# A float32 decoder trunk on one core: first products no longer parted, small steps of feed-forward entries and ends re-ordered, mask building split around the opening

## The chip, the cores and the metric

The kernel runs on one core of one Trainium2 chip. The metric is the device time of one execution in microseconds; "time before" is the median of three runs. Beside the runs there is one profiled execution with its trace, from which all durations come. Engines: PE is TensorE's matmul, PEld its weight load, DVE is VectorE, ACT is ScalarE, POOL is GpSimd, SP is SyncE, which issues most transfers. "L316" is line 316 of the kernel before.

## The reference, cut to what matters

Two layers over 512 tokens of width 1024, in float32. Each layer has two feed-forwards around a token mixer, so there are four feed-forwards:

```
def swiglu(h, w_in, w_out):                      # w_in 1024 x 5632, w_out 2816 x 1024
    gate, up = jnp.split(h @ w_in, 2, axis=-1)
    return (jax.nn.silu(gate) * up) @ w_out

for l in range(DEPTH):                           # DEPTH = 2
    x = x + 0.5 * swiglu(rms_norm(x, ffn1_norm[l]), ffn1_w_in[l], ffn1_w_out[l])
    h = rms_norm(x, mix_norm[l]) @ w_mix_in[l]
    ...                                          # short convolution, HGRN2, forgetting attention
    x = x + y @ w_mix_out[l]
    x = x + 0.5 * swiglu(rms_norm(x, ffn2_norm[l]), ffn2_w_in[l], ffn2_w_out[l])
```

## The kernel before, in words

**Precision.** Every float32 operand is kept as two parts, a rounded high part (`hi`, `xh`) and the remainder (`lo`, `xl`), both of the type float32r. A product of two operands is three matmuls (`mm3`): hi x high at L316, hi x low at L322, lo x high at L323. The high part is a ScalarE copy, the low part a VectorE subtraction.

**A feed-forward** (`ffn`) treats the 2816 hidden columns in 22 blocks of 128. The first four (six in the first feed-forward) are "covered": computed directly with 512-column matmuls (`stream_steps`, weights through `granule` and `parted`), while the norm is finished. The rest goes through `halved`, a Strassen-like scheme in which each 2 x 2 block product takes seven products instead of eight. A unit `("I", w)` is two input blocks of the gate and the up matrix, with products in the order `ORDER_IN = P1, P2, P6, P5, P7, P3, P4`; a unit `("O", ...)` is an output product for a finished chunk of hidden blocks. Each product is 24 matmuls of 256 columns. `CHUNKS` are blocks 0 to 7, 8 to 15 and 16 to 21; `plan` writes down the order of all products and when each load, DMA addition, `total` (a VectorE sum) and `moving` part is done.

**Order in `halved`.** For product number n the loop issues its matmuls (`product`), then `prepare` for product n + 3 (ScalarE high part, L784; the VectorE low part, L786, is kept for later as `rest`), then what is done with the finished bank, then `rest()`, for the last chunk the rounding of the hidden values (L934 on ScalarE, L935 on VectorE), then `run(n)` (the plan's steps; sums at L772) and what `self.entry` holds for n. `A`, `V`, `G` and `S` chain these instructions (`follow`), so ScalarE, VectorE and the queues take them in the order written; the matmuls are chained too (`keep`). Of the bank work: P1 is copied off at L886, P2 subtracted at L889, P6 copied off at L895 (in feed-forwards with an entry this copy, L870, already stands ahead of `prepare`), P5 copied at L898, P7 added at L901, P3 at L904; P4's product gives the hidden values. P1, P6, P7 and P4 of a unit use one bank.

**Parted products.** The first matmul of P1 is split into two of 128 columns for the covered chunk's first unit and the first unit of each later chunk.

**Entry** (`enter`, three of four feed-forwards): it interleaves the direct matmuls with the norm and with the halves of x for P1 to P7 (`high` at L606, `low` at L609 or L611). What does not fit is left in `self.entry` under the product number after which it is issued.

**Opening** (`cover` with `open_stream`, first feed-forward): x is loaded, turned by TensorE (L1686), scaled (`scaled`, L389 and L390) and multiplied with the first weights (L1749), whose parts are made at L1705 and L1706. `idle` issues small matmuls on zeros (L1723). `build_consts` makes the masks for the mixer on VectorE; it stands after `open_stream` in the program, unchained, and the scheduler that orders the unchained instructions puts its steps wherever it expects room. The norm's sum is at L419 and L428.

**Way out** (`way_out`, last feed-forward): the last chunk's hidden blocks times `w_out`, 512 columns at a time into banks that already hold x; the very last tile is halved into two of 256 columns.

Of the kernel before, what the change touches and what calls it, by code (L numbers as in the profile page):

```python
# [23 lines left out]
P = 128  # L24
# [17 lines left out]

SKEW_HELD, SKEW_MOVING = 16, 48
EPS = 1e-6
CH = 64
# [111 lines left out]
class Trunk:  # L157
# [8 lines left out]
    def __init__(self, ctx, tc):  # L166
# [20 lines left out]
        self.tab, self.tab_users, self.loaded = None, [], None  # L187
        self.chain = {}

    def build_consts(self, scratch):  # L190
# [35 lines left out]
        nc.vector.tensor_tensor(later, ftf, ptf, op=ALU.is_gt)  # L226
        a = scratch(F32)[:, :P]
        b = scratch(F32)[:, :P]
        for l in range(1, 7):
            nc.vector.tensor_scalar(a, xf, scalar1=float(2 ** (l - 1)), scalar2=None, op0=ALU.is_ge)  # L230
            nc.vector.tensor_scalar(b, xf, scalar1=float(2**l), scalar2=None, op0=ALU.is_lt)
            nc.vector.tensor_mul(a, a, b)
            for par in range(2):
                r = slice(CH * par, CH * par + CH)
                nc.vector.tensor_mul(self.lmask[r, l - 1, :], a[r, r], later[r, r])

        nc.vector.tensor_scalar(self.maskb, later, scalar1=-1e30, scalar2=None, op0=ALU.mult)

        nc.vector.tensor_tensor(self.utri[:, :P], ftf, ptf, op=ALU.is_ge)
        of = scratch(F32)[:, P:]  # L240
        nc.vector.memset(of, 1.0)
        nc.vector.tensor_copy(self.utri[:, P:], of)

# [35 lines left out]

    def granule(self, parts, kk, ahead=True, skew=0, keep=False, queued=False):  # L280
# [30 lines left out]

    def mm3(self, acc, ah, al, bh, bl, first, last, parted=False, keep=False):
        nc = self.nc
        n = bh.shape[-1]
        for c in (slice(0, n // 2), slice(n // 2, n)) if parted else (slice(0, n),):
# [4 lines left out]
            if keep:  # L320
                self.follow("p", i)
        nc.tensor.matmul(acc, ah, bl, start=False, stop=False, skip_group_check=True)  # L322
        i = nc.tensor.matmul(acc, al, bh, start=False, stop=last, skip_group_check=True)  # L323
        if keep:
# [5 lines left out]

    def stream_steps(self, jobs, parts_of, act, nk, mid=None, pre=None, given=None, queued=False):
        k = 0
        while k < nk:
# [3 lines left out]
            if pre is not None:  # L337
                pre(k)
            skew = SKEW_MOVING if jobs[0][2] is not None and jobs[0][0].shape[-1] < T else 0
            keep = given is not None and given(k)  # L340
            rows = self.granule(parts_of(k, kk), kk, pre is None, skew, keep, queued)
            if keep:
                yield
            end = k + kk == nk
            order = (
# [143 lines left out]
    def cover(self, fp, w_in, covered, begin, then):  # L489
        nc = self.nc  # L490
        x, gain, logits = begin
        for f in range(0, covered, 2):
# [20 lines left out]
            if opening:  # L513
                self.open_stream(x, gain, fp, parts, jobs)
            else:
                self.stream([(*j, None) for j in jobs], parts, self.xact, KD, queued=f == 2)
            if opening:
                nt = iter(["xh4", "xl4", "xh5", "xl5", "xh6", "xl6", "r2", "r3", "r4", "r5"])
                self.build_consts(lambda dt: fp.tile([P, T], dt, tag=next(nt), name=self.n("c")))
                norm()  # L520
# [36 lines left out]
    def enter(self, fp, w_in, then):  # L557
# [74 lines left out]
        def values(f, i):  # L632
# [107 lines left out]
    def halved(self, fp, w_in, w_out, covered):  # L740
# [67 lines left out]
        def product(u, p, bank, start, stop, parted):  # L808
            hi, lo = parts.pop((u, p))
            xh, xl = self.xc[p] if u[0] == "I" else mov[u[1][0], p]  # L810
            for i in range(2):
                acc, c = bank[:, i * H : (i + 1) * H], slice(i * P, (i + 1) * P)
                for k in range(4):
                    self.mm3(
                        acc, hi[:, k, c], lo[:, k, c], xh[:, k, :], xl[:, k, :],
                        start and i == 0 and k == 0, stop and i == 1 and k == 3,
                        parted and i == 0 and k == 0, True,
                    )

# [30 lines left out]
        used = {"I": 0, "O": 0}  # L850
        work = {}

# [4 lines left out]
        for n, (kind, w, p) in enumerate(seq):  # L857
# [3 lines left out]
            if p in new:  # L861
# [3 lines left out]
                u, p, acc, p in new, p in ("P2", "P3", "P4"),  # L865
                kind == "I" and p == "P1" and w in (covered, *(f0 for f0, _ in CHUNKS)),
            )
            if kind == "I" and p == "P6" and self.entry and w == covered:
                work[u, "g2"] = g2 = tmp("g2")
                A(nc.scalar.activation(g2, acc, AF.Copy, scale=-1.0))  # L870
# [35 lines left out]
            else:  # L906
# [8 lines left out]
                else:  # L915
# [13 lines left out]
                    self.hh.append(hh)  # L929
                    self.hl.append(hl)  # L930
            if rest is not None:
                rest()
            if kind == "I" and p == "P4" and w >= CHUNKS[2][0]:
                A(nc.scalar.copy(hh, y))  # L934
                V(nc.vector.tensor_sub(hl, y, hh))  # L935
# [701 lines left out]
    def way_out(self, w_out, out, f0, nf):  # L1637
        nc = self.nc
        for dg in range(2):
            banks = self.next4()  # L1640
            jobs = []
            for i, bk in enumerate(banks):
                t = slice(i * P, (i + 1) * P)
                for q in range(4):
# [12 lines left out]

            self.stream(jobs, parts, self.last_hidden, nf)
            for n, (bk, c, t, _) in enumerate(jobs):
                o = self.res.tile([P, T], F32, tag=f"x{(4 * dg + n) % 8}", name=self.n("xo"))  # L1660
# [8 lines left out]

    def open_stream(self, x, gain, fp, parts, jobs):  # L1670
        nc = self.nc
# [30 lines left out]

        def part(s3, hl, j):
            hi, lo = (hl[:, a + 512 * j : a + 512 * j + 512] for a in (0, 1024))
            A(nc.scalar.copy(hi, s3[:, j, :]))  # L1705
            V(nc.vector.tensor_sub(lo, s3[:, j, :], hi))  # L1706
            return hi, lo
# [3 lines left out]
        V(nc.vector.memset(zeros, 0.0))  # L1711
        A(nc.scalar.dma_start(rows, gain.rearrange("(k p) -> k p", p=P)))
        self.gain = self.const.tile([P, KD], F32, tag="gain", name=self.n("gain"), bufs=2)
# [13 lines left out]
        A(nc.scalar.copy(self.gain, gb[:, :KD]))  # L1727
        idle(2)
        turn(0)
        idle(2)  # L1730
        for k in range(0, KD, 2):
# [5 lines left out]
            wh = []  # L1737
            def make(j):
                self.norm_part(k + j, fp, xb[k + j], 0)
                wh.append(part(*w, j))  # L1740

# [83 lines left out]
```

## Time and profile before

| | us |
|---|---|
| median of 3 runs | 1816.66 (1815.56 to 1819.09) |
| profiled execution | 1815.31 |
| its span in the trace | 1813.2 |
| TensorE matmul busy | 1801.3 (99%) |
| VectorE busy | 1461.3 (81%) |
| ScalarE busy | 1001.0 (55%) |
| HBM read, over the span | 223.98 MB, 125 GB/s |

Timeline rows are: start in the span, duration, engine, line, operation, out<-in, shapes, count. A bracket at the end gives the engine's idle time before it and what ended it. The ends of matmuls are modelled: one of 256 columns is shown with 0.28 us although the next can start 0.11 us after it. Starts are what to read.

The first feed-forward takes the span up to about 340 us (its halved stage from 76.8 to 306.8), then the mixer to about 578, the second feed-forward to about 910 (halved stage from 627.7 to 876.8); the second layer follows in the same way, with halved stages from 953.5 and 1523.3, and the last feed-forward ends the span.

### The profile page before, as it was taken

How to read it: one execution, taken by the hardware profiler on the slowest of the kernel's cores; microseconds unless marked ns; L12 is line 12 of the kernel's file. 1: busy time of each engine (PE TensorE's matmuls, PEld its weight loads, DVE VectorE, ACT ScalarE, POOL GpSimd, SP SyncE). 2: the span in 40 equal slices, each digit the busy share in tenths (PEclk: the TensorE clock that was granted, in tenths of full speed). 3: DMA queues.
4: the chain of work that ended last, by engine and by line, in shares of the span. 5: the costliest groups of instructions: out<-in, count | busy, mean ns of one | idle time of the engine just before them, and what ended most of it. 6: DMA issues, size and time to landing. Idle time of an engine off the chain costs nothing.

```text
span 1813.2 us, 34777 instructions
## 1 busy us (share of the span) xinstructions
PE 1801.3 (99%) x14281; PEld 1682.8 (93%) x14281; DVE 1461.3 (81%) x2048; ACT 1001.0 (55%) x1434; POOL 170.3 (9%) x172
## 2 busy tenths in 40 slices
PE   9999999999999999999999999999999999999999
PEld 7899999899878899999889999998998788999997
DVE  9889787676887898889678887976868878888883
ACT  5455555464775565555445555555547755555551
POOL 0011120100000001112001111201000000020210
PEclk9999999999999999999999999999999999999999
DMA  6768783233323757868275787823233237687762
GB/s 197 186 135 191 179 175 96 74 79 85 87 82 105 216 136 161 197 159 168 82 207 130 163 193 192 163 68 79 77 90 86 82 102 212 163 158 192 158 134 93
DMA packets 243934, 250.94 MB, mean 138 GB/s; under 512 B 18456, under 2 KB 229152, under 8 KB 243776
## 3 DMA queue, kind: packets, MB, share of 16 engines
q1 hardware_dynamic: 189872, 182.38, 33.3%
q0 software_dynamic: 53600, 66.09, 22.8%
q8 instruction: 112, 1.84, 0.4%
q14 instruction: 46, 0.38, 0.1%
q10 hardware_dynamic: 304, 0.27, 0.0%
HBM read 223.98 MB, written 2.10 MB: 125 GB/s over the span
## 4 chain that ended last, share of the span: by engine, by line
PE 91%; DVE 5%; ACT 3%; issue 1%; DMA 0%; SPq 0%; ACTq 0%; DVEq 0%
PE mm L316 13%; PE mm L323 13%; PE mm L322 13%; PE sc L323 6%; PE sc L316 6%; PE sc L322 6%; PE pt L316 6%; PE pt L322 6%; PE pt L323 6%; PE po L316 4%; PE po L322 4%; PE po L323 4%; PE po L1581 1%; PE pt L1623 1%; ACT hl L305 1%
## 5 line engine op out<-in xcount | busy, mean ns | idle before, releaser
L784 ACT CAST hl<-w 128x1024 fp32r<-128x1024 f32 x322 | 337.1, 1049 | 318.2 <-PE mm L323 78.1
L786 DVE TENSOR_TENSOR hl<-w,hl 128x1024 fp32r<-128x1024 f32 x322 | 392.6, 1222 | 85.4 <-ACT hl L784 85.3
L306 DVE TENSOR_TENSOR hl<-st,hl 128x512 fp32r<-128x512 f32 (+2 forms) x188 | 161.6, 860 | 100.7 <-ACT hl L305 99.8
L305 ACT CAST hl<-st 128x512 fp32r<-128x512 f32 (+2 forms) x188 | 141.8, 754 | 176.8 <-PE po L323 62.3
L316 PE MATMUL mm<-xc,hl 128*128 128x256 f32 (+1 forms) x732 | 201.6, 276 | 0.5 <-ACT g L895 0.5
L323 PE MATMUL mm<-xc,hl 128*128 128x256 f32 x728 | 201.4, 277 | 0.0
L322 PE MATMUL mm<-xc,hl 128*128 128x256 f32 x728 | 201.4, 277 | 0.0
L323 PE MATMUL sc<-xc,hl 128*128 128x256 f32 x528 | 146.3, 277 | 0.0
L316 PE MATMUL sc<-xc,hl 128*128 128x256 f32 (+1 forms) x530 | 146.3, 277 | 0.0
L322 PE MATMUL sc<-xc,hl 128*128 128x256 f32 x528 | 146.2, 277 | 0.0
L316 PEld LDWEIGHTS mm<-xc,hl 128*128 128x128 f32 x732 | 137.4, 188 | 0.9 <-ACT g L895 0.7
L323 PEld LDWEIGHTS mm<-xc,hl 128*128 128x128 f32 x728 | 136.7, 188 | 0.1
L322 PEld LDWEIGHTS mm<-xc,hl 128*128 128x128 f32 x728 | 136.7, 188 | 0.0
L322 PE MATMUL pt<-xc,hl 128*128 128x256 f32 x480 | 133.0, 277 | 0.0
L316 PE MATMUL pt<-xc,hl 128*128 128x256 f32 (+1 forms) x484 | 133.0, 276 | 0.0
L323 PE MATMUL pt<-xc,hl 128*128 128x256 f32 x480 | 132.8, 277 | 0.0
L316 PE MATMUL mm<-x,hl 128*128 128x512 f32 x272 | 107.4, 395 | 0.0
L323 PE MATMUL mm<-x,hl 128*128 128x512 f32 x272 | 106.5, 392 | 0.4 <-DVE hl L306 0.4
L322 PE MATMUL mm<-x,hl 128*128 128x512 f32 x272 | 106.4, 391 | 0.0
L316 PEld LDWEIGHTS sc<-xc,hl 128*128 128x128 f32 x530 | 99.6, 188 | 0.2
L323 PEld LDWEIGHTS sc<-xc,hl 128*128 128x128 f32 x528 | 99.3, 188 | 0.1
L322 PEld LDWEIGHTS sc<-xc,hl 128*128 128x128 f32 x528 | 99.1, 188 | 0.0
(514 smaller groups left out, 5604.9 us busy)
## 6 DMA issues: line engine op xcount, KB each, us to landing
w<-in_ffn_w_in_dram SPq DMA_DIRECT2D x140, 512.0 KB
w<-in_ffn_w_out_dram SPq DMA_DIRECT2D x64, 512.0 KB
w<-in_ffn_w_out_dram POOLq DMA_DIRECT2D x56, 512.0 KB, 9.0
st<-in_w_mix_in_dram SPq DMA_DIRECT2D x88, 256.0 KB
st<-in_ffn_w_in_dram SPq DMA_DIRECT2D x70, 256.0 KB
w<-in_ffn_w_in_dram POOLq DMA_DIRECT2D x35, 512.0 KB, 8.2
w<-S POOLq DMA_DIRECT2D x35, 512.0 KB, 4.7
st<-in_ffn_w_out_dram SPq DMA_DIRECT2D x24, 512.0 KB
```

The source lines that it names most:

```text
L305: a = nc.scalar.copy(hi, src[:, c : c + w])
L306: b = nc.vector.tensor_sub(lo, src[:, c : c + w], hi)
L316: i = nc.tensor.matmul(acc[:, c], ah, bh[:, c], start=first and c.start == 0, stop=False, skip_group_check=True,)
L322: nc.tensor.matmul(acc, ah, bl, start=False, stop=False, skip_group_check=True)
L323: i = nc.tensor.matmul(acc, al, bh, start=False, stop=last, skip_group_check=True)
L784: A(nc.scalar.copy(hi, src))
L786: return lambda: V(nc.vector.tensor_sub(lo, src, hi))
L1581: nc.tensor.matmul(self.ob[:, t0 + u * P : t0 + 2 * P], V[:, j, h % 4].rearrange("p a d -> p (a d)"), part[:, j, u:, :].rearrange("p i t - ...
L1623: nc.tensor.transpose(tb[:, j * P : (j + 1) * P], p[:, j * P : (j + 1) * P], self.ident)
```

## The change

- No product is parted any more (`PARTED = ()`).
- Entry: P4's high part is still made after product 3, but its low part after product 4's bank work and ahead of that product's `rest()` (`self.between`). In that P4 the matmul with the low part of x (hi x low) comes last of each three (`lows`). The clearing of the last direct bank and the values from it come one product later (13 and 14 instead of 12 and 13).
- The copy of P6 ahead of `prepare` for the covered unit also in the first feed-forward.
- Last chunk: the hidden values are rounded four products later, behind an output product; the last ones at once as before.
- Way out: the last tile is halved in its last granule only (`ending`), and that granule's weights lie at another offset (`skew`).
- Opening: `build_consts` is a generator. Its first part (tables, `maskb`, `utri`) is issued ahead of the opening's loads, its second part, the six masks, after `open_stream` and behind the low part of the first weights. A mask takes two instructions on 64 columns instead of five on 128 and 64. The first weights' high part is made on VectorE, behind the tables. One `idle` fewer. The first granule of the next stream (`queued`, k = 0) is chained behind the opening on ScalarE and VectorE.

```diff
+PARTED = ()
...
     def build_consts(self, scratch):
...
+        y = scratch(F32)[:, :CH]
+        for par in range(2):
+            r = slice(CH * par, CH * par + CH)
+            nc.vector.tensor_mul(y[r, :], xf[r, r], later[r, r])
+        nc.vector.tensor_scalar(self.maskb, later, scalar1=-1e30, scalar2=None, op0=ALU.mult)
+        nc.vector.memset(self.utri[:, P:].bitcast(F32), 1.0)
+        i = nc.vector.tensor_tensor(self.utri[:, :P], ftf, ptf, op=ALU.is_ge)
+        self.tables = i.ins.name
+        yield
+        both = [scratch(F32)[:, :CH] for _ in range(2)]
         for l in range(1, 7):
-            nc.vector.tensor_scalar(a, xf, scalar1=float(2 ** (l - 1)), scalar2=None, op0=ALU.is_ge)
-            nc.vector.tensor_scalar(b, xf, scalar1=float(2**l), scalar2=None, op0=ALU.is_lt)
-            nc.vector.tensor_mul(a, a, b)
-            for par in range(2):
-                r = slice(CH * par, CH * par + CH)
-                nc.vector.tensor_mul(self.lmask[r, l - 1, :], a[r, r], later[r, r])
+            b = both[l % 2]
+            i = nc.vector.tensor_scalar(b, y, scalar1=float(2**l), scalar2=None, op0=ALU.is_lt)
+            self.tc.add_manual_dep(i.ins, self.first_low, NOSYNC, reason="given order")
+            nc.vector.scalar_tensor_tensor(
+                out=self.lmask[:, l - 1, :], in0=y, scalar=float(2 ** (l - 1)), in1=b,
+                op0=ALU.is_ge, op1=ALU.mult,
+            )
...
     def granule(...):
-            hi, lo = self.parted(st[:, : kk * c], 1 if ahead else kk, skew, keep)
+            hi, lo = self.parted(st[:, : kk * c], 1 if ahead else kk, skew, keep or first)
...
     def mm3(...):
-        nc.tensor.matmul(acc, ah, bl, start=False, stop=False, skip_group_check=True)
-        i = nc.tensor.matmul(acc, al, bh, start=False, stop=last, skip_group_check=True)
+        rest = [(ah, bl), (al, bh)]
+        (a, b), (c, d) = rest[::-1] if lows else rest
+        nc.tensor.matmul(acc, a, b, start=False, stop=False, skip_group_check=True)
+        i = nc.tensor.matmul(acc, c, d, start=False, stop=last, skip_group_check=True)
...
     def enter(...):
-            3: lambda: both("P4"),
+            3: lambda: high("P4"),
...
-            12: lambda: clear(2, 1),
-            13: lambda: values(2, 1),
+            13: lambda: clear(2, 1),
+            14: lambda: values(2, 1),
         }
+        self.between = {4: lambda: lows["P4"]()}
...
     def halved(...):
-                kind == "I" and p == "P1" and w in (covered, *(f0 for f0, _ in CHUNKS)),
+                kind == "I" and p == "P1" and w in PARTED,
             )
-            if kind == "I" and p == "P6" and self.entry and w == covered:
+            if u == ("I", covered) and p == "P6":
...
+            if n in self.between:
+                self.between.pop(n)()
             if rest is not None:
                 rest()
             if kind == "I" and p == "P4" and w >= CHUNKS[2][0]:
+                final = w + 2 == CHUNKS[2][0] + CHUNKS[2][1]
+                rounded.append((n if final else n + 4, y, hh, hl))
+            if rounded and n >= rounded[0][0] and (kind == "O" or rounded[0][0] == n):
+                _, y, hh, hl = rounded.pop(0)
                 A(nc.scalar.copy(hh, y))
                 V(nc.vector.tensor_sub(hl, y, hh))
...
     def way_out(...):
-                cuts = (0, T) if i < 3 or dg == 0 else (0, T // 2, T)
-                jobs += [
-                    (bk[:, a:b], slice(a, b), t, True) for a, b in zip(cuts, cuts[1:])
-                ]
+                jobs.append((bk, slice(0, T), t, True))
...
+            last = jobs[:3] + halved if dg else jobs
+            self.stream(jobs, parts, self.last_hidden, nf, ending=last)
...
     def open_stream(...):
+            if first:
+                i = nc.vector.tensor_copy(hi, s3[:, j, :])
+                self.tc.add_manual_dep(i.ins, self.tables, NOSYNC, reason="given order")
+                V(i)
+            else:
+                A(nc.scalar.copy(hi, s3[:, j, :]))
...
         V(nc.vector.memset(zeros, 0.0))
+        next(consts)
...
-        idle(2)
+        idle(1)
         turn(0)
         idle(2)
```

`stream_steps` puts the jobs of `ending` in place of its own for the last granule. `product` passes `lows` for P4 of the covered unit where `self.entry` still holds something.

More of the change, by code (lines that the diff above doesn't have):

```diff
@@ L277, in follow, with granule @@
         self.chain[engine] = i.ins.name
-    def granule(self, parts, kk, ahead=True, skew=0, keep=False, queued=False):
+    def granule(self, parts, kk, ahead=True, skew=0, keep=False, queued=False, first=False):
         nc = self.nc
@@ L310, in parted, with mm3 @@
         return hh, ll
-    def mm3(self, acc, ah, al, bh, bl, first, last, parted=False, keep=False):
+    def mm3(self, acc, ah, al, bh, bl, first, last, parted=False, keep=False, lows=False):
         nc = self.nc
@@ L517, in cover @@
             if opening:
[L518 to L519 removed]
+                for _ in consts:
+                    pass
                 norm()
@@ L817, in product @@
                         parted and i == 0 and k == 0, True,
+                        u == ("I", covered) and p == "P4" and bool(self.entry),
                     )
@@ L1738, in make @@
             def make(j):
+                first = k + j == 0
+                if first:
+                    pair, low = part(*w, j, True)
                 self.norm_part(k + j, fp, xb[k + j], 0)
-                wh.append(part(*w, j))
+                if not first:
+                    pair, low = part(*w, j)
+                low()
+                wh.append(pair)
             make(0)
```

48 lines of the change are left out of this document (28 added, 20 removed).

## The prediction

> **What bounds the kernel now.** I read the page first, then the waits, then the timeline of TensorE around every place that the diff touches.
>
> ```profile
> PE 1801.3 (99%) x14281; PEld 1682.8 (93%) x14281; DVE 1461.3 (81%) x2048; ACT 1001.0 (55%) x1434; POOL 170.3 (9%) x172
> ```
>
> TensorE is busy 99% of the 1813.2 us span, so nothing on another engine is worth anything unless it lets a matmul start earlier. But a busy share cannot show a matmul that starts a little late, since one lasts longer than its distance to the next. So I go by starts. This is the halved stage of one feed-forward:
>
> ```profile
> 627.73 0.33 PE L316 MATMUL sc<-xc,hl 128*128 128x128 f32 x2
> 628.07 0.28 PE L323 MATMUL sc<-xc,hl 128*128 128x256 f32 x1
> 630.59 0.28 PE L316 MATMUL sc<-xc,hl 128*128 128x256 f32 x1
> ...
> 644.13 0.19 PEld L316 LDWEIGHTS sc<-xc,hl 128*128 128x128 f32 x1
> 644.19 0.33 PE L316 MATMUL sc<-xc,hl 128*128 128x256 f32 x1
> 644.35 0.28 PE L322 MATMUL sc<-xc,hl 128*128 128x256 f32 x1
> ...
> 666.85 0.33 PE L316 MATMUL pt<-xc,hl 128*128 128x128 f32 x2
> ```
>
> A product is 24 matmuls of 256 columns. From 630.59 to 644.19 five of them, 120 matmuls, take 13.60 us: 113.3 ns each, the full pace. From 644.19 to 666.85 eight, 192 matmuls, take 22.66 us: 118.0 ns each. The second stretch begins with a small slip: 644.35 comes 0.16 after 644.19 instead of 0.11, and from then on TensorE runs 4% slower, with no wait shown. It ends at 666.85, where a parted product stands. At 118 instead of 113.3 ns, 192 matmuls lose 0.90 us. The starts show the same in each of the three feed-forwards that begin with an entry. So the kernel has few long waits, and its losses are slips of 0.05 to 0.7 us and this slower pace.
>
> **The change, part by part.** The sum is made against the profiled execution, 1815.3 us (span 1813.2 and 2.1 around it); the median shown is 1816.7, 1.4 above, and I carry that over at the end.
>
> *Parted products.* The first product of the covered chunk and of the two others is parted in each of four feed-forwards: 12. The one at 627.73 takes 2.86 us to 630.59 against 24 x 0.1133 = 2.72: 0.14 lost, no work hidden by it (its two halves are one matmul's columns). Removed: 12 x 0.135 = 1.6 us. The Trainium skill, TensorE: Matmul & The Clock Gate, section Back-to-back issue gap, gives about 81 ns for a sustained 128-column matmul with its weight load: two would cost 49 ns more than our 113, so 0.6 us in all and a sum of 7.0 instead of 8.0; the trace shows 0.14 each and decides. Bounds: 0 (a wait that the second half now covers appears) to 1.6. But a parted product is also what ended the slower pace at 666.85; this returns as a rival.
>
> *Entry: P4's low part.* VectorE, in front of the slip:
>
> ```profile
> 642.20 1.22 DVE L609 SCALAR_TENSOR_TENSOR xc<-xn,xc 128x1024 fp32r<-128x1024 f32 x1
> 643.33 0.68 DVE L901 TENSOR_TENSOR u<-u,sc 128x512 f32<-128x512 f32 x1
> ```
>
> P4 (from 644.19) adds onto the bank that L901 reads for P7, and L901 ends at 644.01, because P4's own low part (L609) stands before it. Its weight load starts at 644.13, only 0.06 ahead of the matmul where the load is otherwise a full 0.11 ahead: that is the slip. The change turns the two round: L901 then runs 642.2 to 642.9, 1.3 us before it is needed, and L609 about 642.8 to 644.0. What is late next is L609: its result is read by P4's hi x low matmul, which `lows` moves from second to third, at 644.19 + 0.23 = 644.42, its load due at 644.31. Margin 0.3 us, 0.1 to 0.2 after the 0.135 that TensorE comes earlier, if VectorE doesn't follow. Behind L609 only the low part of the product after next waits. Gain: 3 x 0.90 = 2.7 us; bounds 0 to 2.7, below zero only in the rival. The moves of `clear(2, 1)` and `values(2, 1)` by one product put four instructions of VectorE behind P4's own results; the banks they empty are next written five products (13 us) later: nothing.
>
> *First feed-forward: P6's copy ahead of the weights' high part.*
>
> ```profile
> 86.98 1.04 ACT L784 CAST hl<-w 128x1024 fp32r<-128x1024 f32 x1
> 87.74 0.28 PE L323 MATMUL mm<-xc,hl 128*128 128x256 f32 x1
> 87.92 0.58 ACT L895 ACTIVATE g<-mm 128x512 f32<-128x512 f32 x1
> 88.56 0.38 PE L316 MATMUL mm<-xc,hl 128*128 128x256 f32 x1 [0.54 <-ACT g L895]
> ```
>
> L895 frees the bank for P7, due at 87.74 + 0.11 = 87.85; it came at 88.56, 0.71 late, and the matmul after it lost another 0.11. Put first, L895 runs 86.98 to 87.56. Gain 0.8. The high part goes 0.5 later; it is for the product after next. Bounds 0.5 to 0.82.
>
> *Ends: rounding of the hidden values four products later.*
>
> ```profile
> 843.03 1.23 DVE L935 TENSOR_TENSOR hh<-y,hh 128x1024 fp32r<-128x1024 f32 x1
> 845.90 1.22 DVE L772 TENSOR_TENSOR S<-w,w 128x1024 f32<-128x1024 f32 x1
> 848.32 1.23 DVE L786 TENSOR_TENSOR hl<-S,hl 128x1024 fp32r<-128x1024 f32 x1 [1.19 <-ACT hl L784]
> ...
> 849.35 0.28 PE L316 MATMUL sc<-xc,hl 128*128 128x256 f32 x1
> 849.60 0.39 PE L323 MATMUL sc<-xc,hl 128*128 128x256 f32 x1
> 855.08 0.28 PE L316 MATMUL pt<-xc,hl 128*128 128x256 f32 x1
> ```
>
> L786 ends at 849.55 and L323 at 849.60 waits for it; the chain behind it is L935, the sum L772, ScalarE's copy, L786. Two products from 849.35 to 855.08 take 5.73 us against 5.44: 0.29 lost, and alike at the three other ends. Without L935 in front (1.14 from start to start) the sum and L786 come 1.1 earlier, ahead of need. The rounding, with its ScalarE copy, now stands behind an output product's additions, where the next low part has over a product in hand. Gain 4 x 0.25 = 1.0; bounds 0 to 1.15. The last rounding stays where it was.
>
> *Opening, start.* In the fence first TensorE and ScalarE, then VectorE.
>
> ```profile
> 1.22 1.65 PE L1723 MATMUL mm<-z 128*128 128x128 f32 x6 [1.22 <-DVE z L1711]
> 4.02 0.90 PE L1686 MATMUL mm<-ident,xs 128*128 128x128 f32 x4
> 4.76 0.61 PE L1723 MATMUL mm<-z 128*128 128x128 f32 x4
> 4.96 0.69 ACT L389 ACTIVATE x<-mm,gain 128x512 fp32r<-128x512 f32 x1 [1.44 <-PE mm L1686]
> 5.54 0.61 ACT L1705 CAST hl<-st 128x512 fp32r<-128x512 f32 x1
> 6.20 0.73 PE L1749 MATMUL sc<-x,hl 128*128 128x512 f32 x2 [0.84 <-ACT hl L1705]
> ...
> 2.64 0.36 DVE L242 CAST utri<-c 128x384 fp32r<-128x384 f32 x1
> 4.28 0.22 DVE L230 TENSOR_SCALAR c<-c 128x128 f32<-128x128 f32 x1
> 4.55 0.28 DVE L239 TENSOR_TENSOR utri<-c,c 128x128 fp32r<-128x128 f32 x1
> 5.07 0.45 DVE L235 TENSOR_TENSOR lmask<-c,c 64x64 uint8<-64x64 f32 x2
> ```
>
> The first product waits for ScalarE: x, then the weights' high part, done 6.15. With the high part on VectorE only x is left. One `idle` fewer is two small matmuls (`idle(3)` is the six from 1.22), which start 0.21 apart here: 0.43 us, so x is done at 4.96 + 0.69 - 0.43 = 5.22 (at 5.65 if the transposes wait for x's load instead). VectorE must first finish the tables: L239 ends at 4.83, less 0.27 for the cast that goes (L242), less 0.27 for two mask steps (4.28 to 4.55), plus 0.45 for the two multiplies that join the masks (as L235), so 4.74; then the copy, 0.48 scaled from L242 or 0.68 at most: 5.2 to 5.4. Start at 5.3 instead of 6.20: gain 0.9, bounds 0.4 to 0.95. Behind the copy queue x's low part and the weights' low part, wanted four and eight matmuls later (0.9, 1.8 us, and four transposes): covered.
>
> *Opening, end.*
>
> ```profile
> 26.69 1.22 DVE L306 TENSOR_TENSOR hl<-st,hl 128x1024 fp32r<-128x1024 f32 x1
> 27.83 0.74 DVE L390 SCALAR_TENSOR_TENSOR x<-po,gain,x 128x512 fp32r<-128x512 f32 x1
> 27.96 0.50 PE L323 MATMUL mm<-x,hl 128*128 128x512 f32 x1 [0.39 <-DVE hl L306]
> 28.62 0.50 PE L1749 MATMUL sc<-x,hl 128*128 128x512 f32 x1
> 33.79 0.69 DVE L419 TENSOR_TENSOR sh<-sqa,sh 128x512 fp32r<-128x512 f32 x1
> 34.53 0.50 PE L428 MATMUL po<-sh,ones_mean 128*128 128x512 f32 x1
> ```
>
> The next stream's first weights (L306) stand on VectorE ahead of the opening's last x (L390); TensorE waits for the one (0.55), then the other, and for the norm's sum (0.32), with 0.1 to restart after each: 1.3 us. The change puts that granule behind the opening's own chain on ScalarE and VectorE, and the masks fall from 30 instructions to 12, at about 0.2 us each (L230, L235) some 3 us less of VectorE. Then the opening's products run through. Next late is the norm's sum: L419 follows the same chain, and TensorE reaches it 1.8 us earlier. I take 0.9 of 1.3; bounds -0.5 (the granule's low part is wanted before it is done) to 1.3.
>
> *Last tile.* Halved columns only in the last granule: the same columns, 24 matmuls of 256 become 12 of 512, twice as long each. No difference but some slips: 0.1. The other offset of that granule's weights moves addresses only: 0.
>
> Sum: 1.6 + 2.7 + 0.8 + 1.0 + 0.9 + 0.9 + 0.1 = 8.0 us; profiled execution 1807.3, median 1816.7 - 8.0 = 1808.7.
>
> **The rivals.** *A just-late wait sets the slower pace, and nothing ends it.* With no parted products, a slip of 0.05 us in an entry (P4's low part later than 644.3) or at P7 in the first feed-forward (L895 misses 87.74) puts TensorE at 118 ns until the next disturbance; with the ends repaired that may be the end of the chunk, some 200 us on. Price: 200 x 4.7/113.3 = 8.3 us for each feed-forward. It decides from one such stretch: it eats the whole gain. In three entries: 3 x 8.3 = 25, so 1833 or so; in one, 1817. For it: 192 matmuls at 118 ns that ended at a parted product. Against: the margins of 0.1 to 0.3 us, and that after the longer stall at 88.56 the pace was back (seen in the starts). Chance 0.22, half of it one stretch.
>
> *The slips are only exchanged.* P4's slip stays in one form or another but the pace recovers at the next product; the opening gives half: about 4 us, 1812.5. Chance 0.15.
>
> *It doesn't do what it says:* the planner's orders come out as before where it matters, and only the parted products go: 1.6 us, 1815, within 0.2%. Chance 0.05.
>
> *The clock.* The four transposes from 4.02 stand 0.21 us apart, the small matmuls from 4.76 0.11: the clock is full from about 4.7, 3.4 us after 1.22. If leaving out 0.43 us of work at the start puts this off by as much again, the first products from 5.3 to 8.1 run at half pace and lose 1.4 us: 1810.1. Chance 0.03. The Trainium skill, TensorE: Matmul & The Clock Gate, section What's actually happening, says that the clock is released after a window of about 3.4 us of sustained work; by that rule this opening is as I read it, and the trace agrees.
>
> **How the numbers follow.** The forecast, 1808.7, has 0.55; its own range is 1806.0 to 1812. One slower stretch reaches 1817, the exchange 1812.5, so 1806.0 to 1817.5 leaves out the wide form of the first rival and some of the tails. A measurement of this kernel can tell about 0.2%, 3.6 us, so faster means below 1813: the forecast, the clock and most of the exchange, 0.70. Within 0.2%: the third rival, the rest of the exchange and part of the single stretch, 0.10. Slower: the rest, 0.20.
>
> **What would show it.** Right: no 128-column matmuls from `xc`; in every entry products of 2.72 us from P4 on; no wait of L316 for L895 near 87; first L1749 near 5.3; no wait for L786 at the four ends. Wrong: products of 2.83 us over tens of microseconds, or a new wait for L609, or a first product that waits for VectorE's tables.

## The result: 0.8% slower, and where it lies

The changed kernel takes 1830.18 us (median of 6 runs, 1829.34 to 1839.84) against 1817.26 for the kernel before in the same session: ratio 1.0077, 95% interval 1.0064 to 1.0091. The forecast was 1808.7, range 1806.0 to 1817.5. The profiled execution takes 1830.67 us with a span of 1828.9, 15.7 more than before's 1813.2. (The median of the kernel before lay between 1816.7 and 1824.9 in the sessions of this study, so every ratio is taken within one session.)

In the page of the changed kernel TensorE is as busy as it was:

```profile
PE 1819.1 (99%) x14255; PEld 1701.0 (93%) x14255; DVE 1457.4 (80%) x2032; ACT 1000.3 (55%) x1433; POOL 170.4 (9%) x172
```

TensorE is busy 17.8 us longer with 14255 matmuls instead of 14281. Waits do not explain it: what is left of the span beside TensorE's busy time falls from 11.9 to 9.8 us. The starts say where the time goes. In what follows a slot is the time from the start of one matmul to the start of the next (0.11 us for 256 columns), and the pace is the mean of many slots. This is TensorE at the beginning of the second feed-forward's halved stage in the changed kernel (L322, L330 and L331 are the L316, L322 and L323 of before):

```profile
634.57 0.39 PE L331 MATMUL po<-x,hl 128*128 128x512 f32 x1
634.80 0.28 PE L322 MATMUL sc<-xc,hl 128*128 128x256 f32 x1
634.92 0.28 PE L330 MATMUL sc<-xc,hl 128*128 128x256 f32 x1
...
637.62 0.28 PE L322 MATMUL sc<-xc,hl 128*128 128x256 f32 x1
...
648.93 0.28 PE L322 MATMUL pt<-xc,hl 128*128 128x256 f32 x1
...
651.76 0.28 PE L322 MATMUL sc<-xc,hl 128*128 128x256 f32 x1
```

The direct matmuls of 512 columns end at 634.57, and the first halved product, 634.80 to 637.62, takes 2.83 us instead of 2.72. Six products to 651.76 take 16.96 us, 117.8 ns for each matmul. There is no slip ahead of it: the stage *starts* at the slower pace, and in this stage nothing ends it. The table has the time of each halved stage, from its first matmul to the first one behind the stage:

| us | first | second | third | fourth | rest of the span |
|---|---|---|---|---|---|
| before | 229.99 | 249.11 | 249.11 | 249.10 | 835.9 |
| after | 237.44 | 257.25 | 249.49 | 249.48 | 835.2 |
| after less before | +7.45 | +8.14 | +0.38 | +0.38 | -0.7 |

In after, the slower pace holds for 2016 matmuls of the first stage, for all 2184 of the second (433 and 1750, with one slot of 0.14 us between), and for the first 433 of the third and fourth. In the third and fourth stage such a slot of 0.14 us, 0.03 longer than its neighbours, brings the full pace back; in the second it did not. The third stage's, where the matmul reads the sum of hidden values `m` that VectorE ends at 1019.60:

```profile
1019.73 0.30 PE L330 MATMUL sc<-m,hl 128*128 128x256 f32 x1
1019.87 0.28 PE L331 MATMUL sc<-m,hl 128*128 128x256 f32 x1
```

At 4.45 ns each the slower matmuls lose 22.55 us. The stages grew by 16.35 in all, so the rest of the edits earned 6.2 us inside them.

The repaired places in the changed kernel are, in this order, VectorE at P4, ScalarE at P6's copy, and VectorE at an end:

```profile
649.23 0.68 DVE L919 TENSOR_TENSOR u<-u,sc 128x512 f32<-128x512 f32 x1
649.83 1.22 DVE L625 SCALAR_TENSOR_TENSOR xc<-xn,xc 128x1024 fp32r<-128x1024 f32 x1
...
86.80 0.58 ACT L888 ACTIVATE g<-mm 128x512 f32<-128x512 f32 x1
87.27 2.03 ACT L801 CAST hl<-w 128x1024 fp32r<-128x1024 f32 x2
...
854.62 0.68 DVE L943 TENSOR_TENSOR y<-g,sc 128x512 f32<-128x512 f32 x1
858.09 1.22 DVE L789 TENSOR_TENSOR S<-w,w 128x1024 f32<-128x1024 f32 x1
860.50 1.22 DVE L803 TENSOR_TENSOR hl<-S,hl 128x1024 fp32r<-128x1024 f32 x1 [1.19 <-ACT hl L801]
866.25 1.22 DVE L959 TENSOR_TENSOR hh<-y,hh 128x1024 fp32r<-128x1024 f32 x1
```

P7's addition (L919) now stands ahead of P4's low part (L625), P6's copy (L888) ahead of the high part (L801), and the rounding (L959) behind the sum (L789); no matmul waits at any of these places. The opening shows TensorE, then ScalarE, then VectorE:

```profile
4.60 1.06 PE L1761 MATMUL mm<-z 128*128 128x128 f32 x4
5.58 1.22 PE L1793 MATMUL sc<-x,hl 128*128 128x512 f32 x2
6.60 1.05 PE L1793 MATMUL pt<-x,hl 128*128 128x512 f32 x2
8.16 1.18 PE L1793 MATMUL sc<-x,hl 128*128 128x512 f32 x2
9.16 0.64 PE L1793 MATMUL pt<-x,hl 128*128 128x512 f32 x2
...
4.84 0.69 ACT L401 ACTIVATE x<-mm,gain 128x512 fp32r<-128x512 f32 x1 [1.33 <-PE mm L1712]
4.95 0.43 DVE L1732 CAST hl<-st 128x512 fp32r<-128x512 f32 x1 [0.37 <-DMA st<-in_ffn_w_in_dram]
```

In the kernel before, the second pair of matmuls stood here:

```profile
6.77 0.62 PE L1749 MATMUL pt<-x,hl 128*128 128x512 f32 x2
```

The first product comes at 5.58 instead of 6.20, but its two matmuls of 512 columns take 1.02 us where before's two took 0.57 (6.20 to 6.77). I read that as half the clock. Before had the clock in full from about 4.7; here it comes past 9. The twelfth of these matmuls starts 4.75 us behind the first, in before 3.09.

### The profile page after: what moved, and what is told of

It reads as the page before. It is cut to its first block, busy times and chain, and to the rows that moved or that the text cites. A ratio compares the mean times of both kernels' runs of the same rounds, so it can differ in the third digit from the quotient of the medians.

```text
span 1828.9 us, 34708 instructions
## 1 busy us (share of the span) xinstructions
PE 1819.1 (99%) x14255; PEld 1701.0 (93%) x14255; DVE 1457.4 (80%) x2032; ACT 1000.3 (55%) x1433; POOL 170.4 (9%) x172
## 4 chain that ended last, share of the span: by engine, by line
PE 93%; DVE 3%; ACT 3%; issue 1%; DMA 0%; SPq 0%; ACTq 0%
PE mm L322 13%; PE mm L331 13%; PE mm L330 13%; PE sc L331 6%; PE sc L330 6%; PE sc L322 6%; PE pt L331 6%; PE pt L322 6%; PE pt L330 6%; PE po L322 4%; PE po L331 4%; PE po L330 4%; PE po L1605 1%; PE pt L1647 1%; ACT hl L311 1%
## 5 line engine op out<-in xcount | busy, mean ns | idle before, releaser
L801 ACT CAST hl<-w 128x1024 fp32r<-128x1024 f32 x322 | 337.0, 1049 | 337.6 <-PE mm L331 87.5
L322 PE MATMUL mm<-xc,hl 128*128 128x256 f32 x728 | 203.1, 279 | 0.0
L331 PE MATMUL mm<-xc,hl 128*128 128x256 f32 x728 | 203.1, 279 | 0.0
L330 PE MATMUL mm<-xc,hl 128*128 128x256 f32 x728 | 203.1, 279 | 0.0
L322 PE MATMUL sc<-xc,hl 128*128 128x256 f32 x528 | 147.4, 279 | 0.0
L331 PE MATMUL sc<-xc,hl 128*128 128x256 f32 x528 | 147.4, 279 | 0.0
L330 PE MATMUL sc<-xc,hl 128*128 128x256 f32 x528 | 147.4, 279 | 0.0
L330 PEld LDWEIGHTS mm<-xc,hl 128*128 128x128 f32 x728 | 138.5, 190 | 0.1
L322 PEld LDWEIGHTS mm<-xc,hl 128*128 128x128 f32 x728 | 136.6, 188 | 0.1
L331 PEld LDWEIGHTS mm<-xc,hl 128*128 128x128 f32 x728 | 136.7, 188 | 0.0
L322 PE MATMUL pt<-xc,hl 128*128 128x256 f32 x480 | 134.0, 279 | 0.0
L330 PE MATMUL pt<-xc,hl 128*128 128x256 f32 x480 | 134.0, 279 | 0.0
L331 PE MATMUL pt<-xc,hl 128*128 128x256 f32 x480 | 134.0, 279 | 0.0
L322 PE MATMUL mm<-x,hl 128*128 128x512 f32 x272 | 107.3, 395 | 0.0
L330 PE MATMUL mm<-x,hl 128*128 128x512 f32 x272 | 106.5, 391 | 0.0
L331 PE MATMUL mm<-x,hl 128*128 128x512 f32 x272 | 106.4, 391 | 0.0
L322 PEld LDWEIGHTS sc<-xc,hl 128*128 128x128 f32 x528 | 99.9, 189 | 0.1
L330 PEld LDWEIGHTS sc<-xc,hl 128*128 128x128 f32 x528 | 99.7, 189 | 0.1
L331 PEld LDWEIGHTS sc<-xc,hl 128*128 128x128 f32 x528 | 99.1, 188 | 0.0
```

Source lines behind the costliest of these rows:

```text
L322: i = nc.tensor.matmul(acc[:, c], ah, bh[:, c], start=first and c.start == 0, stop=False, skip_group_check=True,)
L330: nc.tensor.matmul(acc, a, b, start=False, stop=False, skip_group_check=True)
L331: i = nc.tensor.matmul(acc, c, d, start=False, stop=last, skip_group_check=True)
L801: A(nc.scalar.copy(hi, src))
```

## The experiments

**1 to 4: the parted products.** The first puts the twelve back into the changed kernel, the second takes them out of the kernel before, the third parts only the first product of each stage.

```diff
# 1: after
-                kind == "I" and p == "P1" and w in PARTED,
+                kind == "I" and p == "P1" and w in (covered, *(f0 for f0, _ in CHUNKS)),
# 2: before
-                kind == "I" and p == "P1" and w in (covered, *(f0 for f0, _ in CHUNKS)),
+                False,
# 3: after
-                kind == "I" and p == "P1" and w in PARTED,
+                kind == "I" and p == "P1" and w == covered,
```

> The changed kernel with the twelve parted products put back, all else as changed. Theory (pace): a halved stage begins at 118 ns a matmul when 256-column matmuls follow the 512-column ones undisturbed, and a parted product brings TensorE to 113.3 ns; the rest of the change gains its 5 to 7 us. Expected 1810 to 1812 us, all stretches of 118 ns gone. Rival (another part of the change, the order lo x high before hi x low, the later rounding or the VectorE order, makes the matmuls slower): stays near 1828 us, with 118 ns from the first P1 or from P4 of the entry on.

> The kernel before with no parted product, nothing else. Theory (pace): four halved stages of 230 to 250 us begin at 118 ns; what ends it is left to chance (the 0.7 us stall at 88 us in the first, the slip at P4 in the three entries), so 1 to 4% of them is lost: 1822 to 1855 us. Rival (the parted products only cost 0.13 us each and another part of the change did the harm): 1815.7 us, 1.6 faster than before.

> The changed kernel with only the first product of each halved stage parted (four instead of none). Theory (pace): once at 113.3 ns, TensorE stays there until something slips, and the changed kernel has no slips in the stages: 1809.5 to 1811 us, 1 us less than with twelve. Rival (the pace falls off by itself and the later parted products renew it): stretches of 118 ns from the second chunk on, 1815 to 1828 us.

Measured: 1 takes 1813.02 (11 runs), ratio 0.9975 (0.9965 to 0.9984); 2 takes 1839.83 (4 runs), ratio 1.0123 (1.0109 to 1.0138); 3 takes 1827.23 (9 runs, 1819.66 to 1834.6), ratio 1.0041 (1.0022 to 1.0061). So taking out the twelve alone, with no other edit, costs 22 us (1817.83 in the same session); putting them back into the changed kernel takes 18 away (the ratio falls from 1.0077 to 0.9975). In 2, TensorE at the start of the second stage:

```profile
627.71 0.28 PE L316 MATMUL sc<-xc,hl 128*128 128x256 f32 x1
627.83 0.28 PE L322 MATMUL sc<-xc,hl 128*128 128x256 f32 x1
...
630.54 0.28 PE L316 MATMUL sc<-xc,hl 128*128 128x256 f32 x1
...
633.36 0.28 PE L316 MATMUL sc<-xc,hl 128*128 128x256 f32 x1
```

2.83 us a product from the first matmul on, and so to the end: three whole stages of 2184 matmuls at 117.8 ns, 9.7 us each. Only in the first stage did something end it, after 11 us: a wait of 0.37 us for ScalarE's L895 at 88.3. Run 3 missed what was expected of it. It starts each stage at 113.3 ns, but loses the pace at a wait on VectorE of 0.36 us (92.4, 684.2 and 1585.9) until the stage ends; behind the same wait in the third stage (1017.0) it keeps it.

Is it the splitting of a product, or just a short matmul? Experiment 4, too, treats only the first product of each stage. It leaves that product whole and puts one more matmul of 128 columns ahead of it, whose result is overwritten:

```diff
+        if parted:
+            i = nc.tensor.matmul(
+                acc[:, : n // 2], ah, bh[:, : n // 2], start=True, stop=False,
+                skip_group_check=True,
+            )
+            self.follow("p", i)
+        for c in (slice(0, n),):
```

> The changed kernel with an extra 128-column matmul ahead of the first product of each halved stage, whose result the unparted first matmul overwrites. Theory (pace set by any short matmul that shifts weight loads against matmuls): as with the parted one, 1810 to 1811 us and 113.3 ns from there on. Rival (it is the splitting of that one matmul, its waits or its two halves of the bank, that counts): 118 ns as in the changed kernel, about 1830 us.

```profile
627.60 0.22 PE L322 MATMUL sc<-xc,hl 128*128 128x128 f32 x1
627.65 0.33 PE L328 MATMUL sc<-xc,hl 128*128 128x256 f32 x1
...
630.45 0.28 PE L328 MATMUL sc<-xc,hl 128*128 128x256 f32 x1
...
633.17 0.28 PE L328 MATMUL sc<-xc,hl 128*128 128x256 f32 x1
```

L322 is here the added matmul and L328 the whole one. From 630.45 to 633.17 is 2.72: the full pace, and so at the start of all four stages. The time was 1827.53 (10 runs, 1819.07 to 1835.62), ratio 1.0043, as in 3 and far from the 1810 to 1811 expected: the pace was again lost at a wait of 0.36 us (677.3 and 1579.0), and kept behind the same wait at 94.7 and 1010.1. A short matmul sets the full pace; that a product is parted is not what matters.

**5, 6: what remains when they are back.** Run 1 had new waits, since TensorE now comes earlier: 0.37 us for P7's addition at 92.75, and 0.16 to 0.35 for the sum of hidden values `m` at 676.3, 1005.5 and 1575.2. Behind the first of these, 910 matmuls ran at 117.8 ns, 4.05 us lost. That pace had begun 5.7 us ahead of the wait, at a slot of 0.15 us (670.38); in the last feed-forward it began at such a slot too (1569.20), and there the wait of 0.16 us ended it. Run 5 puts three small VectorE steps one product later, run 6 gives the `idle` back as well.

```diff
# 5, on top of 1
-                    if n in (1, 3):
-                        finish(n // 2)
+                    if n in (1, 4):
+                        finish(n // 4)
-            13: lambda: clear(2, 1),
-            14: lambda: values(2, 1),
+            14: lambda: clear(2, 1),
+            15: lambda: values(2, 1),
# 6, on top of 5
-        idle(1)
+        idle(2)
```

> The changed kernel with the twelve parted products back, and three steps moved that came too early on VectorE: clear(2, 1) and values(2, 1) after products 14 and 15 instead of 13 and 14, and in the first feed-forward the clearing of the last direct banks after product 4 instead of 3. Theory (any short wait of TensorE can drop it to 118 ns; the waits left in the kernel with twelve parted products come from VectorE being busy with these clears): no wait for the moving part m (0.16 to 0.35 us near 676, 1005 and 1575) nor for P7's addition (0.37 near 92), no stretch of 118 ns behind them: 1808 to 1811 us, runs closer together. Rival (the drop is random): the stretches come all the same, 1812 to 1818 us.

> As the last, with the left-out idle put back ahead of the first transposes. Theory (the missing 0.43 us of small matmuls put off the full clock, so that the first products ran 0.43 us apart instead of 0.23): the 512-column products 0.23 us apart from the first on, the first halved product at 75.0 to 75.4 us, 0.5 to 1 us less than without: 1807.5 to 1810 us. Rival (the point at which the clock comes is chance): the same spread, first halved product between 75.5 and 77.7 us.

Measured: 1812.0 (12 runs), ratio 0.9971 (0.9956 to 0.9986), and 1812.03 (11 runs), ratio 0.997 (0.9955 to 0.9985). The wait at 92.75 is gone; those for `m` stay, 0.41 us each, and in these two traces the full pace holds behind all six. With the `idle` back, no matmul of 512 columns ran at half pace and the first halved product came at 75.6 instead of 76.6 us: 1 us in the trace, too little to be seen in the medians.

**7, 8, 11, 12: where the weights lie.** The parts of the halved weights lie 16 elements into their buffer (`SKEW_HELD`). 7, 8 and 12 are the changed kernel with 0, 48 and 32, 11 is the sixth kernel with 0. One execution each.

> The changed kernel with the weights' parts of the halved stages 64 bytes lower in their buffers (offset 0 instead of 16 elements), nothing else. Theory (the pace is a matter of time, the weight loads against the matmuls): the same two paces, 118 ns from the first P1 on, about 1830 us. Rival (a clash of addresses between weights and moving data): another share of 118 ns, none (about 1808 us) or all (about 1846 us).

> As the last with offset 48 instead of 16. Theory: the same two paces, about 1830 us. Rival: another share of 118 ns, about 1808 or 1846 us, or a third pace.

> The sixth kernel with the held weights at offset 0 instead of 16. With no parted product, offset 0 gave 120.0 ns for each halved matmul instead of 117.8. If the offset sets only the size of the slower pace and a short matmul brings back the full pace whatever the offset, the halved stages run at 113.3 ns behind each parted product: 1812 to 1820. If the offset takes the full pace away altogether, 120.0 ns throughout and about 1812 + 8700 x 6.7 ns = 1870.

> The changed kernel, with no parted product, with the held weights at offset 32 instead of 16. Offsets 16 and 48 gave 117.8 ns, 0 gave 120.0. If the pace goes by the distance between the held and the moving operand's offsets (48 less the held one's: 32, 0, 48 so far), 16 is a new distance and may give a third pace; if only offset 0 is special, 117.8 ns and 1830 to 1849; if a half step of 32 is like 0, 120.0 ns and 1850 to 1865.

| offset | parted | ns for each halved matmul | us |
|---|---|---|---|
| 16 (after) | no | 117.8 | 1830.67 |
| 48 | no | 117.8 | 1848.59 |
| 0 | no | 120.0 | 1865.05 |
| 32 | no | 120.0 | 1866.95 |
| 0 | yes | 120.0 | 1867.61 |

Run 7 in its second halved stage:

```profile
649.98 0.28 PE L322 MATMUL pt<-xc,hl 128*128 128x256 f32 x1
...
650.34 0.28 PE L322 MATMUL pt<-xc,hl 128*128 128x256 f32 x1
```

Three matmuls in 0.36 us. At 0 and 32 the pace is 120.0 ns. At 0, parted products do not help: in 11 the 120.0 ns come back at once behind each. At 48 and 32 they were not tried. So the full pace was seen only at an offset of 16, beside a second, stable one, and which of the two holds there is decided by small events. My theory that time alone decides fell with run 7.

**9, 10: the sum and the entry.** 9 was to put the sum `m` one product earlier, but the planner chose the same place: its instructions are those of 6 on every engine. It is a repeat. 10 is 6 with the entry's order as before.

```diff
# 9
-            a = at["O", (c, 1), ORDER_OUT[i - 2]] if i > 1 else n0["P2"] - 3
+            a = at["O", (c, 1), ORDER_OUT[i - 2]] if i > 1 else n0["P2"] - 4
# 10 (and P4 without lows)
-            3: lambda: high("P4"),
+            3: lambda: both("P4"),
-        self.between = {4: lambda: lows["P4"]()}
+        self.between = {}
```

> The sixth kernel (parted products back, later clears, the idle block back) with the planner allowed to put the moving half of P2 one product earlier. The sixth kernel's trace had three waits of 0.41 us plus 0.11 to restart for VectorE's sum m at L755, at 675.8, 1000.9 and 1570.6. If the sum is late only because it is issued too late, the three waits go and the time falls by 3 x 0.5 = 1.5 us, to about 1810.5 where the sixth had 1812.0. If VectorE is simply full there, the wait stays or moves to the next sum or weight part, and the time is the sixth's within 0.5 us. If a small wait in its place sets the slower pace (117.8 ns), 8 us are lost for each chunk in which it does: 1820 or more.

> The sixth kernel with the entry's order as in the kernel before: both parts of P4's half of x after product 3, no part in between, the low matmul in its usual second place. If the entry's order is what ended the slip at P4, the slip of 0.05 us is back in the three entries and with it eight products of 192 matmuls at 118 ns until the next parted product, 3 x 0.9 = 2.7 us: about 1814.7 against the sixth's 1812.0. If the order is worth nothing (the waits were only exchanged), 1812 to 1812.5, the sums at L755 on time again because VectorE and TensorE are back in their old distance.

Measured: 9 takes 1816.56 (12 runs, 1812.53 to 1822.41), ratio 0.9996 (0.9984 to 1.0009), though 6 with the same instructions took 1812.03 in another session (ratio 0.997). 10 takes 1814.16 (10 runs), ratio 0.998 (0.9968 to 0.9992). In 10 P4's slip is back in all three entries, 0.05 us each:

```profile
643.18 0.33 PE L322 MATMUL sc<-xc,hl 128*128 128x256 f32 x1
643.35 0.28 PE L330 MATMUL sc<-xc,hl 128*128 128x256 f32 x1
...
969.22 0.33 PE L322 MATMUL mm<-xc,hl 128*128 128x256 f32 x1
969.38 0.28 PE L330 MATMUL mm<-xc,hl 128*128 128x256 f32 x1
```

After the first, 191 matmuls ran at 117.8 ns up to the parted product at 665.84, as before; after the second, and a third like it, the pace stayed at 113.3. The stages took 249.36, 248.49 and 248.49 us where 9 took 248.43 to 248.44 in the first two. So the new order is worth 0.05 to 0.9 us an entry, as it falls.

**13 to 15: what starts the slower pace where there are parted products.** 13 makes the sum `m` really one product earlier, 14 parts one more product behind each chunk's first output product, where that wait stands, 15 is 6 once more, all in one session.

```diff
# 13
-            loose.append((a, min(n0[p] - 3, last if p == "P7" else N), ("moving", c, p)))
+            loose.append((a, min(n0[p] - (4 if p == "P2" else 3), last if p == "P7" else N), ("moving", c, p)))
# 14
+                or n > 0 and seq[n - 1][0] == "O" and seq[n - 1][1][1] == 0 and seq[n - 1][2] == "P2",
```

> The sixth kernel with the moving half of each chunk's first output product (the sum m at L755) really made one product earlier, 2.7 us, where it had come 0.41 us too late at 675.8, 1000.9 and 1570.6. If these three waits are what starts the slower pace in the executions that took 4 or 8 us longer, the trace shows none of the three waits, the fastest execution falls by 3 x 0.5 = 1.5 us to about 1810.5, and far fewer executions lie 4 us or more above the fastest: a median within 2 us of the fastest. If the longer executions have another start, they are as many as in the sixth and ninth kernels (14 of 23 over 3 us above their fastest).

> The sixth kernel with one more parted product behind each chunk's first output product, the product that has the wait of 0.41 us: 8 more short pairs. If they cost 0.14 us each and the wait starts the slower pace in some executions, the fastest is 8 x 0.14 = 1.1 us above the sixth's and the executions 4 us longer are gone: a median within 2 us of the fastest, about 1813.5. If the slower pace does not start there, the scatter stays and the median is 1 us above that of the repeat.

> The sixth kernel once more, unchanged, in the same session as the two others. The sixth had a median of 1812.0 and the ninth, whose instructions turned out to be the same on every engine, 1816.6. If the difference is executions in which a chunk runs at the slower pace (910 matmuls at 117.8 instead of 113.3 ns: 4.05 us), the times again lie in groups 4 us apart, from 1811 to 1821, and the median is anything between 1812 and 1817.

| us | median | all runs | ratio |
|---|---|---|---|
| 13 | 1818.99 | 12, 1815.46 to 1823.34 | 0.9974 (0.9961 to 0.9987) |
| 14 | 1812.72 | 6, 1812.21 to 1814.30 | 0.9943 (0.9929 to 0.9957) |
| 15 | 1815.69 | 8, 1811.74 to 1819.83 | 0.9954 (0.9939 to 0.9969) |

13 was expected to gain and lost. Its three waits are gone; VectorE and then TensorE show what came in their place:

```profile
678.14 1.23 DVE L803 TENSOR_TENSOR hl<-w,hl 128x1024 fp32r<-128x1024 f32 x1 [0.52 <-ACT hl L801]
...
679.35 0.28 PE L330 MATMUL pt<-xc,hl 128*128 128x256 f32 x1
679.47 0.34 PE L331 MATMUL pt<-xc,hl 128*128 128x256 f32 x1
679.64 0.28 PE L322 MATMUL pt<-xc,hl 128*128 128x256 f32 x1
...
783.76 0.28 PE L331 MATMUL po<-m,hl 128*128 128x256 f32 x1
783.88 0.33 PE L322 MATMUL pt<-xc,hl 128*128 128x128 f32 x2
```

The weights' low part is done at 679.37; L331, which reads it, starts at 679.47, and the matmul behind it 0.17 later instead of 0.11. From 679.64 to 783.76 there are 885 matmuls at 117.8 ns, 3.93 us lost, up to the next parted product; likewise at 1008 and 1581. That is the just-late wait of my rival, three times in one execution: a slip of 0.06 us costs 65 times its length. (The execution profiled is one of the two slowest of the twelve.)

A long wait may start the slower pace or not. The wait for `m` in 6, and in 15:

```profile
675.28 0.28 PE L322 MATMUL mm<-m,hl 128*128 128x256 f32 x1
675.81 0.38 PE L330 MATMUL mm<-m,hl 128*128 128x256 f32 x1 [0.25 <-DVE m L755]
...
678.54 0.28 PE L322 MATMUL pt<-xc,hl 128*128 128x256 f32 x1
...
681.26 0.28 PE L322 MATMUL sc<-xc,hl 128*128 128x256 f32 x1
```

```profile
1000.65 0.28 PE L322 MATMUL sc<-m,hl 128*128 128x256 f32 x1
1001.17 0.39 PE L330 MATMUL sc<-m,hl 128*128 128x256 f32 x1 [0.24 <-DVE m L755]
...
1003.99 0.28 PE L322 MATMUL mm<-xc,hl 128*128 128x256 f32 x1
...
1006.81 0.28 PE L322 MATMUL mm<-xc,hl 128*128 128x256 f32 x1
```

The same wait within 0.01 us; behind it 2.72 us a product in 6 and 2.82 in 15, there for 910 matmuls, 4.04 us. It is rare in the traces kept: of fifteen such waits in 5, 6, 9, 10 and 15, this is the only one with the slower pace behind it. 14 keeps the waits (0.41 us each) and puts short matmuls behind them: all of its six runs lie within 2.1 us, where 15 and 9 with 20 runs spread over 8 and 10. That suggests that most of the scatter of 6, 9 and 15 is the slower pace behind that wait; with six runs, and no trace of a long execution of 6 or 9, it is not shown. 14 is the version to keep: its slowest run is faster than the fastest of the kernel before in any session (1814.30 against 1814.97).

## Why the prediction was wrong, step by step

**The step that failed is the first term, the parted products.** It took their cost, 12 x 0.14 us, from the row of one of them, and set nothing against it but waits that their removal might uncover, so its bounds were 0 and a gain of 1.6. The 1.6 was earned, and 22.55 us were lost, because the short matmul was what set the full pace at the start of every stage (2 and 4 show it) and restored it in later chunks (before, 10 and 13). The sign had been in the prediction's own rows: the stage at 630.59 ran at 113.3 ns behind a parted product, and the stretch at 118 ended at the next. I read the second as the end of a disturbance and never asked what the first product would do without it. What came is the sign of being wrong that the prediction had named: products of 2.83 us over tens of microseconds.

**The first rival was right that a slower pace would hold for want of parted products, and in its price, and wrong in its trigger.** I made it wait for a slip and gave it 0.22, on the strength of margins of 0.1 to 0.3 us. These margins held: neither after nor 6, which runs at the full pace, has a slip at P4 or at the place of P6's copy. The pace was lost all the same, from the first product on. That its 1833 for three feed-forwards lies near the 1830 measured is luck: two stages ran slow as a whole and two for their first 433 matmuls. Where a kernel does have parted products, a slip can be the trigger (13, and one entry in three of 10).

**The other terms inside the stages held together.** 1.6 + 2.7 + 0.8 + 1.0 = 6.1 us were forecast, and 6.2 came once the pace is set aside. But part of it was lent. With the full pace back, TensorE waits for the sum `m` in three entries (in 6 for 0.41 us, with 0.11 to restart, each time): 1.6 us given back. That is the second rival, slips exchanged, at less than half its size. With the full pace, run 6's stages take 974.6 us in all, 2.7 less than before's 977.3.

**The opening's two terms were eaten by the clock.** The start was forecast at 5.3 and came at 5.58, 0.2 of it waiting for x's load; the end lost its waits but for 0.3 us at the norm's sum (0.08 and twice 0.11 to restart). The first halved product came 0.15 us earlier (76.69 for 76.84), not 1.8. What ate it is the rival called the clock, to which I gave 0.03: forecast 1.4 us, measured 4.75 - 3.09 = 1.66 over the first twelve matmuls. The terms were too large even without it: run 3 has the same opening with the clock in time, and its first halved product comes at 75.54, 1.3 us earlier than in before. With one `idle`, seven of the eight traces show the first two to seven matmuls of 512 columns with 0.58 us or more instead of 0.39 to 0.50; with two, two of nine do (10 and 13, four each). The Trainium skill, TensorE: Matmul & The Clock Gate, section What's actually happening, says that the window is free-running, so that the number of slow matmuls differs from run to run. The traces agree: 0 in 3 and 7 in 4 with the same opening. So the late clock came more often with one `idle` fewer; no run separates how much of it is chance.

**The last tile** was forecast at 0.1; the stretch behind the last stage went from 36.55 to 36.38, 0.17.

## What to carry to other kernels

When TensorE is the bound, compare the spacing of starts with its best value stage by stage: a busy share of 99% hid 22.55 us here. An instruction that looks like a small waste may be what keeps a faster regime; before it goes, look at what the work directly behind it does, and try its removal alone. Where two paces exist, mend waits completely or place a short matmul behind them: a slip of 0.06 us can cost more than a wait of 0.5.

## What the runs showed of the hardware

Matmuls of 256 columns with a new weight load each have two stable paces on this chip, 113.3 and 117.8 ns, with the operands of this kernel at offset 16; at offsets 0 and 32 only 120.0 ns was seen. At offset 16 the faster pace stood behind a matmul of 128 columns in all 124 places of the traces that have one, and the slower one in all eight stages of after and 2 that follow matmuls of 512 columns without one. Other events went either way. A slot of 0.14 us brought the faster pace back in two places of after and not in a third; a wait of 0.16 us (1) and one of 0.37 (2) brought it back; slips of 0.04 to 0.06 and waits of 0.4 sometimes ended it. In the traces a weight load starts 110 ns ahead of its matmul at the faster pace, 114 to 115 at the slower and 117 to 118 at 120.0: each load begins 2 to 4 ns behind the start of the matmul before. Why a stretch keeps its pace, and why the offset matters, stays open.
